# Experts of up to 128 slots: the whole first weight tile of the second product stays float32, not its first half alone

## The chip, the cores and the metric

The kernel runs on one core of a Trainium2 chip. The metric is device time in microseconds (us): the time of one execution, as a median over runs. The profile is one further execution, recorded by the hardware profiler; its times count from its first instruction. PE is the matrix engine (PEld its weight loads), ACT the activation engine, DVE the vector engine, POOL the engine that issues indirect DMAs, SP the one that issues the weight loads.

## What is computed

One layer of a trunk of 1024 tokens of width 1024: a mixer (a recurrence and an attention side by side) and then a mixture of 32 experts, of which each token takes four. The change lies in the experts alone. Their part of the reference, cut to the core:

```python
def expert_block(args):                       # one expert e, a block of its tokens
    tok, gate, e = args
    xb = xt[tok]
    hid = xb @ w1[e] + b1[e]                  # first product, 1024 -> 2 x 1024
    glu = jnp.minimum(hid[:, :1024], 7.0)
    lin = jnp.clip(hid[:, 1024:], -7.0, 7.0)
    act = glu * jax.nn.sigmoid(1.702 * glu) * (lin + 1.0)
    return (act @ w2[e] + b2[e]) * gate[:, None]   # second product, 1024 -> 1024
```

All of it is float32.

## The kernel before

**Tiles and units.** The 32 experts are taken in an order that alternates between well filled and thinly filled ones, so position j (0 to 31) has room for c slots: the even positions 168 down to 136, the odd positions 1 to 25 exactly 128 (thirteen of them), 27 to 31 136. An expert's weights are six tiles of 2 MB: four of w1 (w=1, q=0..3) and two of w2 (w=2, q=0 and 1). The tiles of two experts are interleaved: (j+1,1,0), (j,2,0), (j+1,1,1), (j,2,1), (j+1,1,2), (j+1,1,3), in the notation (position, w, q). They are loaded into four buffers `wraw0` to `wraw3` in turn, by SP, in that order (`w_load`, L1369; line L1380 for w1, L1386 for w2); a load waits until the last reader of the tile four places earlier is done. Each tile is worked off in two halves, h=0 and h=1; a half is a unit.

**Split and native units.** A float32 half tile is split for PE: ACT rounds it to `whi` (L1409, `w_hi`), DVE takes the rest, `wlo = wraw - whi` in bf16 (L1427, `w_lo`). `next_hi` runs three units ahead of PE, `next_lo` two. A unit of the first product (`first`, L1429) is 16 matmuls with `whi` (L1437) and 16 with `wlo` (L1441) into a PSUM tile `hid`, of which there are two; ACT and DVE empty it into `ht` (L1447, L1448). A split unit of the second product (`second`, L1498) is 12 matmuls of 512 columns: `whi` with the two parts `ah` and `al` of the activation, `wlo` with `ab`. `gated` makes `act` and these parts. A native unit (`native`) skips all of that: four matmuls in float32 straight from `wraw` and `act`, which PE runs as eight instructions. Before, the first half of the first w2 tile, (j,2,0) h=0, is native for every expert.

**The gather.** While PE works on an expert, the rows of the next one are found and fetched: one-hot rows times `aux` on PE (L1308), some small DVE steps on `sa` that end in the integer row numbers `si` (L1318), an indirect DMA on POOL into `xg` (L1327), and transposes `xt` on PE (L1344), which stand in PE's order behind unit (j+1,1,1) h=1 for position j+2.

**Order.** The program is recorded unit by unit (`experts`, L1555); a scheduler of the framework then sets the order on each engine, and each engine runs its list in that order. So an instruction that waits holds back all that stands behind it on its engine.

Of the kernel before, what the change touches and what calls it, by code (L numbers as in the profile page):

```python
# [67 lines left out]
def run(*gens):  # L68
    for g in gens:
        for _ in g:  # L70
            pass


class Box:
# [40 lines left out]
class Trunk:  # L115
# [798 lines left out]
    def mix(self, rp, zps, rps, sps, make_pool):  # L914
# [152 lines left out]
        self.ep0 = make_pool[1]()  # L1067
        bank = iter(("sbt", "sbo") * 4)
        run(self.x_transpose(self.xs[0], self.ep0, lambda: sps.tile([128, 512], FT, name="fxt", tag=next(bank), bufs=1)))
        self.next_lo(1)  # L1070
        self.next_hi(2)
# [322 lines left out]
    @staticmethod  # L1394
    def native(u):

        return u.t.w == 2 and u.t.q == u.h == 0

    def w_hi(self, u, pool):
        nc = self.nc  # L1400
# [49 lines left out]
    def gated(self, u, pool):  # L1450

        nc, x = self.nc, u.t.x
        c, part = x.c, 2 * (u.t.q // 2) + u.h
        n1 = self.rest(c)
        glu, lin = (t[:, 2 * u.h:2 * u.h + 2] for t in x.t)
        sg = pool.tile([128, 2, c], FT, name="hs", bufs=1, tag="hs")
        nc.scalar.activation(sg, glu, AF.Sigmoid, scale=ALPHA)
        nc.vector.tensor_scalar(lin, lin, LIMIT + 1.0, 1.0 - LIMIT, op0=OP.min, op1=OP.max)
        yield
        act = pool.tile([128, 2, 128 + n1], FT, name="act", bufs=5, tag="act")  # L1460
        if c < 128 + n1:
            nc.gpsimd.memset(act[:, :, c:], 0.0)
        nc.vector.scalar_tensor_tensor(lin, sg, SIG_MAX, lin, op0=OP.min, op1=OP.mult)
        nc.vector.scalar_tensor_tensor(act[:, :, :c], glu, LIMIT, lin, op0=OP.min, op1=OP.mult)
        x.act.append(act)
        if part == 0:
            x.parts.append(None)
            return
        ah = pool.tile([128, 2, 128], FR, name="ah", bufs=ABUF, tag="ah")
        ab = pool.tile([128, 2, 128], BF, name="ab", bufs=ABUF, tag="ab")  # L1470
        nc.scalar.activation(ah, act[:, :, :128], AF.Copy)
        nc.scalar.activation(ab, act[:, :, :128], AF.Copy)
        yield
        al = pool.tile([128, 2, 128], FR, name="al", bufs=ABUF, tag="al")
        nc.vector.tensor_tensor(al, act[:, :, :128], ah.bitcast(FT), op=OP.subtract)
        x.parts.append((ah, al, ab))

    def second(self, u, pool, psum):


        nc, x, t = self.nc, u.t.x, u.t
        first, last = t.q == u.h == 0, t.q == u.h == 1
        n1 = self.rest(x.c)
        nj = 128 // n1 if n1 else 0
        wd = D // nj if n1 else 0
        if first:
            x.ps = [psum.tile([128, 512], FT, name="ey", bufs=2) for _ in range(2)]
            if n1:
                x.pr = psum.tile([128, 512], FT, name="er", bufs=1)
        i = 2 * t.q + u.h  # L1490
        if self.native(u):
            products = [(x.act[i], t.raw, j) for j in range(2)]
        else:
            ah, al, ab = x.parts[i]
            products = [(a, u.hi, j) for j in range(2) for a in (ah, al)] + [(ab, u.lo, j) for j in range(2)]
        for m, (a, w, j) in enumerate(products):
            for n in range(2):
                nc.tensor.matmul(x.ps[n], a[:, j, :128], w[:, j, n * 512:(n + 1) * 512],  # L1498
                                 start=first and m == 0, stop=last and m == len(products) - 1)
        if n1 and u.h == 1:  # L1500
            for k in range(4):
                a = x.act[2 * t.q + k // 2]
                for g in range(nj):
                    nc.tensor.matmul(x.pr[g * n1:(g + 1) * n1, :wd], a[:, k % 2, 128:], t.raw[:, k, g * wd:(g + 1) * wd],  # L1504
                                     start=t.q == k == 0, stop=t.q == 1 and k == 3)
        if not last:
            return
        y = pool.tile([128, D], FT, name="ey", bufs=1)
        for n in range(2):
            ns = slice(n * 512, (n + 1) * 512)  # L1510
            nc.vector.scalar_tensor_tensor(y[:, ns], x.ps[n], x.gate[:, 0:1], self.g2b[:, ns], op0=OP.mult, op1=OP.mult)  # L1511
        rows = self.out.rearrange("b s d -> (b s) d")
        nc.gpsimd.indirect_dma_start(out=rows, out_offset=bass.IndirectOffsetOnAxis(ap=x.idx[:, 0:1], axis=0),  # L1513
                                     in_=y, in_offset=None, compute_op=OP.add)
        if n1:
            yr = pool.tile([128, wd], FT, name="yr", bufs=1, tag="yr")
            nc.vector.scalar_tensor_tensor(yr, x.pr[:, :wd], x.gate[:, 1:2], self.g2r[n1], op0=OP.mult, op1=OP.mult)
            rests = self.out.rearrange("b s (j d) -> (b s j) d", j=nj)
            nc.gpsimd.indirect_dma_start(out=rests, out_offset=bass.IndirectOffsetOnAxis(ap=x.idx[:, 2:3], axis=0),
                                         in_=yr, in_offset=None, compute_op=OP.add)  # L1520

    def load(self):

        pools = (self.wp, self.wp, self.ep1, self.ep2)
        while self.loaded < len(self.tiles) and (self.loaded < WRAW or self.loaded - WRAW in self.free):
            pool = pools[self.loaded % WRAW]
            if pool is None:
                return
            run(self.w_load(self.tiles[self.loaded], pool))
            self.loaded += 1  # L1530
# [193 lines left out]
def tile_trunk(ctx, tc, ins, out, dbg=None):  # L1724
# [11 lines left out]
    with ExitStack() as pre:  # L1736
# [21 lines left out]
                for tag in ("rwum", "rwT", "rwv", "rwk")]  # L1758
        ada = T.ada(0, sp, sps, iter(big).__next__, "sbt")
        run(take(ada, 8))  # L1760
        xt = next(norms[0])
        w = [T.z_weights(128 * m, zp) for m in (12,)]
# [87 lines left out]
```

## Time and profile before

| | |
|---|---|
| time before, median of 3 runs | 2486.65 us (2483.01 to 2488.38) |
| the profiled execution | 2474.98 us, span 2473.2 us |
| PE busy over the span | 2331.7 us (94%) |
| DVE, ACT busy | 1969.1 us (80%), 1576.0 us (64%) |
| granted PE clock, mean | 0.973 |
| time of one weight load, issue to landing, median | 14.5 us |

The experts fill the span from about 1085 us to the end. There PE is busy nearly all the time, and the loads keep the DMA engines busy too. A busy share is an average; which of the two ends last at a place is read from the waits and the chain.

### The profile page before, as it was taken

What the parts mean: (1) busy time and instruction counts of PE and PEld (TensorE: products, weight loads), DVE (VectorE), ACT (ScalarE), POOL (GpSimd) and SP (SyncE); (2) the same over time, 40 slices, a digit from 0 to 9 for tenths busy, and PEclk for the clock granted to TensorE, in tenths of its full rate; (3) what the DMA queues carried; (4) which work ended last, traced back from release to release, by engine and by line L of the source; (5) the groups of instructions that cost most, each with busy time, mean ns of one, the idle gap of its engine ahead of it and who ended that gap; (6) DMA issues with size and microseconds to landing.
All of it is one profiled execution on the core that took longest, in us unless ns stands there. A gap on an engine that the chain in (4) does not pass through costs nothing.

```text
span 2473.2 us, 49792 instructions
## 1 busy us (share of the span) xinstructions
PE 2331.7 (94%) x19973; PEld 1765.6 (71%) x19973; DVE 1969.1 (80%) x3639; ACT 1576.0 (64%) x2467; POOL 219.5 (9%) x182
## 2 busy tenths in 40 slices
PE   6889999999999799979999999999999999999997
PEld 2456666667676665667887787888788877877875
DVE  5567568669687768678888888989888889899875
ACT  3635556557666646346676676677777777776764
POOL 0000000000000000001121111111111111121111
PEclk9989999999999799979999999999999999999999
DMA  8773343332232312567898898899899999998995
GB/s 300 268 242 114 104 118 105 112 102 83 79 106 77 107 47 93 185 213 273 302 342 279 300 362 312 313 328 363 317 314 334 343 322 323 333 365 300 320 318 158
DMA packets 321006, 579.57 MB, mean 234 GB/s; under 512 B 46526, under 2 KB 110020, under 8 KB 320740
## 3 DMA queue, kind: packets, MB, share of 16 engines
q1 hardware_dynamic: 304768, 532.21, 60.6%
q0 software_dynamic: 14304, 43.53, 7.1%
q8 instruction: 159, 2.61, 0.4%
q10 hardware_dynamic: 1700, 0.61, 0.1%
q14 instruction: 75, 0.61, 0.1%
HBM read 517.69 MB, written 58.61 MB: 233 GB/s over the span
## 4 chain that ended last, share of the span: by engine, by line
PE 70%; DMA 14%; DVE 8%; ACT 5%; issue 3%; SPq 0%; POOL 0%; POOLq 0%; ACTq 0%; DVEq 0%
PE hid L1437 14%; PE ey L1498 14%; DMA wraw<-in_exp_w_dram 8%; PE hid L1441 6%; PE rwps L660 6%; PE zps L336 4%; PE zps L338 3%; PE zps L337 3%; PE er L1504 3%; PE sbo L526 2%; DMA xg<-h2d,si 2%; ACT whi L1409 2%; PE mp L972 1%; PE sbt L523 1%; PE mp L973 1%
## 5 line engine op out<-in xcount | busy, mean ns | idle before, releaser
L1409 ACT ACTIVATE whi<-wraw 128x2048 fp32r<-128x2048 f32 (+1 forms) x361 | 675.2, 1874 | 364.3 <-PE hid L1437 167.3
L1427 DVE TENSOR_TENSOR wlo<-wraw,whi 128x2048 bf16<-128x2048 f32 (+1 forms) x361 | 804.3, 2233 | 118.2 <-PE hid L1441 73.2
L1437 PE MATMUL hid<-X,whi 128*128 128x256 f32 (+7 forms) x4096 | 622.9, 304 | 27.1 <-DVE ht L1448 25.2
L1437 PEld LDWEIGHTS hid<-X,whi 128*128 128x128 f32 x4096 | 560.6, 191 | 62.2 <-issue 44.9
L1441 PE MATMUL hid<-xb,wlo 128*128 128x128 bf16 (+7 forms) x4096 | 300.6, 227 | 0.0
L1441 PEld LDWEIGHTS <-wlo 128*128 128x128 bf16 x4096 | 253.4, 98 | 18.3 <-issue 0.3
L338 PE MATMUL zps<-hhi,zwlo 128*128 128x512 f32 x416 | 247.1, 594 | 0.0
L336 PE MATMUL zps<-hhi,zwhi 128*128 128x512 f32 x416 | 188.8, 454 | 22.1 <-DVE zlast L380 9.6
L337 PE MATMUL zps<-hlo,zwhb 128*128 128x512 bf16 x416 | 168.5, 405 | 1.4 <-DVE hlo L247 1.4
L1447 ACT ACTIVATE ht<-hid,b1r 128x128 f32<-128x128 f32 (+7 forms) x496 | 156.8, 371 | 6.1 <-PE hid L1441 5.9
L1498 PE MATMUL ey<-whi,ah 128*128 128x512 f32 x384 | 142.2, 451 | 0.0
L1448 DVE TENSOR_TENSOR ht<-ht,hid 128x256 f32<-128x256 f32 (+7 forms) x256 | 114.1, 446 | 25.6 <-ACT ht L1447 25.0
L1513 POOL DMA_INDIRECT out_dram<-ey,si x32 | 91.5, 2859 | 410.6 <-DVE ey L1511 409.4
L336 PEld LDWEIGHTS zps<-hhi,zwhi 128*128 128x128 f32 x416 | 82.7, 199 | 54.8 <-issue 22.1
L1498 PE MATMUL ey<-wraw,act 128*128 128x512 f32 x256 | 121.4, 607 | 0.0
L1498 PE MATMUL ey<-whi,al 128*128 128x512 f32 x384 | 120.6, 395 | 0.0
L1327 POOL DMA_INDIRECT xg<-h2d,si x49 | 78.8, 1609 | 406.4 <-PE ey L1498 210.2
L337 PEld LDWEIGHTS <-zwhb 128*128 128x128 bf16 x416 | 42.2, 102 | 93.5 <-issue 88.9
L1498 PE MATMUL ey<-wlo,ab 128*128 128x512 bf16 x384 | 99.6, 382 | 0.0
L514 DVE TENSOR_TENSOR_SCAN se<-se 128x128 f32<-128x128 f32 (+3 forms) x96 | 92.8, 970 | 0.7
L244 ACT ACTIVATE zwhi<-zwraw 128x1024 fp32r<-128x1024 f32 x50 | 52.8, 1055 | 60.3 <-PE zps L336 40.4
L1498 PEld LDWEIGHTS ey<-whi,ah 128*128 128x128 f32 x384 | 69.9, 189 | 28.6 <-issue 14.8
(475 smaller groups left out, 4095.3 us busy)
## 6 DMA issues: line engine op xcount, KB each, us to landing
wraw<-in_exp_w_dram SPq DMA_DIRECT2D x189, 2048.0 KB, 14.5
zwraw<-in_w_in_dram SPq DMA_DIRECT2D x50, 512.0 KB, 4.1
aw<-in_ada_w_dram SPq DMA_DIRECT2D x32, 512.0 KB, 5.7
zr<-zo SPq DMA_DIRECT2D x28, 256.0 KB, 2.3
zs<-zo SPq DMA_DIRECT2D x24, 256.0 KB, 2.1
nx<-in_x_dram SPq DMA_DIRECT2D x8, 512.0 KB, 7.1
awh<-in_ada_w_dram SPq DMA_DIRECT2D x8, 512.0 KB, 4.6
mx<-in_x_dram SPq DMA_DIRECT2D x16, 256.0 KB, 3.2
```

Source lines behind the costliest of these rows:

```text
L336: nc.tensor.matmul(ps, hi[:, k], self.hhi[:, k, s], start=k == 0, stop=False)
L337: nc.tensor.matmul(ps, hb[:, k], self.hlo[:, k, s], start=False, stop=False)
L338: nc.tensor.matmul(ps, lo[:, k], self.hhi[:, k, s], start=False, stop=k == ND - 1)
L514: nc.vector.tensor_tensor_scan(er, er, er, initial=carry, op0=OP.add, op1=OP.bypass)
L660: self.nc.tensor.matmul(out[hs], lhsT[hs], rhs[hs], start=start, stop=stop)
L1409: nc.scalar.activation(dst[:, k], src[:, k], AF.Copy)
L1427: nc.vector.tensor_tensor(dst[:, k], src[:, k], hi[:, k], op=OP.subtract)
L1437: nc.tensor.matmul(ps[:, b, :2 * c], u.hi[:, k, b * 128:(b + 1) * 128], x.X2[:, k].rearrange("p a c -> p (a c)"), start=k == 0, stop=False)
L1441: nc.tensor.matmul(ps[:, b, :c], u.lo[:, k, b * 128:(b + 1) * 128], x.xb[:, k, :], start=False, stop=k == ND - 1)
L1447: nc.scalar.activation(dst[:, b], ps[:, b, c:2 * c], AF.Identity, bias=x.bias[:, f + b:f + b + 1])
L1448: nc.vector.tensor_tensor(dst, dst, ps[:, :, :c], op=OP.add)
L1498: nc.tensor.matmul(x.ps[n], a[:, j, :128], w[:, j, n * 512:(n + 1) * 512], start=first and m == 0, stop=last and m == len(products) - 1)
```

## The change

A new function `nat(c)` says how many halves of w2 stay native: two for an expert with up to 128 slots, one otherwise. For the thirteen odd positions 1 to 25, unit (j,2,0) h=1 becomes native: its `whi` on ACT, its `wlo` on DVE, the `ah`, `ab` (ACT) and `al` (DVE) of that quarter of the activation are not made, and its 12 matmuls become four float32 ones, eight instructions. The slice of `t.raw` picks the half of the tile.

```diff
+def nat(c):
+
+    return 2 if c <= 128 else 1
...
     def native(u):
 
-        return u.t.w == 2 and u.t.q == u.h == 0
+        return u.t.w == 2 and 2 * u.t.q + u.h < nat(u.t.x.c)
...
         x.act.append(act)
-        if part == 0:
+        if part < nat(c):
             x.parts.append(None)
             return
...
         if self.native(u):
-            products = [(x.act[i], t.raw, j) for j in range(2)]
+            products = [(x.act[i], t.raw[:, 2 * u.h:2 * u.h + 2], j) for j in range(2)]
```

Two places of the order, both around the second products of position 9 (128 slots) while position 10 (160 slots) has its first. ACT before; `wraw_16257` is tile (9,2,0), `wraw_16259` tile (10,1,1), the four `ht` of 128 columns empty the two units of (9,1,3):

```order
L1457 ACTIVATE hs<-ht 128x256
L1409 ACTIVATE whi<-wraw_16257 128x2048
L1447 ACTIVATE ht<-hid,b1r 128x128 x4
L1409 ACTIVATE whi<-wraw_16259 128x2048
L1471 ACTIVATE ah<-act 128x256
L1472 ACTIVATE ab<-act 128x256
L1457 ACTIVATE hs<-ht 128x256
L1447 ACTIVATE ht<-hid,b1r 128x160 x2
L1409 ACTIVATE whi<-wraw_16259 128x2048
```

ACT at the same place after the change, where tile (10,1,1) is `wraw_16181`:

```order
L1462 ACTIVATE hs<-ht 128x256
L1452 ACTIVATE ht<-hid,b1r 128x128 x4
L1462 ACTIVATE hs<-ht 128x256
L1476 ACTIVATE ah<-act 128x256
L1477 ACTIVATE ab<-act 128x256
L1414 ACTIVATE whi<-wraw_16181 128x2048
L1476 ACTIVATE ah<-act 128x256
L1477 ACTIVATE ab<-act 128x256
L1452 ACTIVATE ht<-hid,b1r 128x160 x2
L1414 ACTIVATE whi<-wraw_16181 128x2048
```

No `whi` stands ahead of the four `ht` any more; an `hs` and an `ah` and `ab` have moved ahead of the first `whi` of tile (10,1,1). DVE before, a little later, from the first `wlo` of tile (10,1,1) to the row numbers of the gather for position 11:

```order
L1427 TENSOR_TENSOR wlo<-wraw_16259,whi 128x2048
L1475 TENSOR_TENSOR al<-act,ah 128x256
L1463 SCALAR_TENSOR_TENSOR ht<-hs,ht 128x256
L1448 TENSOR_TENSOR ht<-ht,hid 128x320
L1464 SCALAR_TENSOR_TENSOR act<-ht 128x256
L1311 COPY sa<-xt 128x5
L1427 TENSOR_TENSOR wlo<-wraw_16259,whi 128x2048
L1475 TENSOR_TENSOR al<-act,ah 128x256
L1448 TENSOR_TENSOR ht<-ht,hid 128x320
...
L1296 TENSOR_SCALAR oh<-slot,keyr 128x160
L1316 TENSOR_TENSOR sa<-sa 128x1
L1318 CAST si<-sa 128x1
```

DVE there after the change:

```order
L1432 TENSOR_TENSOR wlo<-wraw_16181,whi 128x2048
L1453 TENSOR_TENSOR ht<-ht,hid 128x320
L1480 TENSOR_TENSOR al<-act,ah 128x256
L1432 TENSOR_TENSOR wlo<-wraw_16181,whi 128x2048
L1453 TENSOR_TENSOR ht<-ht,hid 128x320
L1316 COPY sa<-xt 128x5
L1301 TENSOR_SCALAR oh<-slot,keyr 128x160
L1319 SCALAR_TENSOR_TENSOR sa<-sa 128x1
L1320 TENSOR_TENSOR sa<-sa 128x1
L1301 TENSOR_SCALAR oh<-slot,keyr 128x160
L1321 TENSOR_TENSOR sa<-sa 128x1
L1323 CAST si<-sa 128x1
```

An `al` and the gating steps have moved ahead of this stretch; the copy of `sa` has moved behind both `wlo`, and one more `oh` stands ahead of `si`. On PE and SP the order is as before but for the replaced matmuls.

## Rows read from the trace of the kernel before

**Rows 1.** Busy time by window: busy us (count) of each engine, PE clock, DMA share, GB/s

```profile
1500.00:1600.00 100.00, 97.97 (x865) 81.44 (x864) 91.92 (x130) 73.24 (x102) 12.95 (x7) 1.00 0.93 326
```

**Rows 2.** Waits of PE, 1157 to 2202 us: total us, times, longest

```profile
PE hid L1437 <- DVE ht L1448: 22.6, 19, 2.7
PE xt L1344 <- DMA xg<-h2d,si: 3.2, 5, 1.1
```

**Rows 3.** Chain that ended last, in order of time: start, us, what

```profile
1506.21 11.15 DMA wraw<-in_exp_w_dram
1517.45 1.91 ACT whi L1409
1520.47 2.58 PE hid L1437 x16
...
1617.77 7.39 DMA xg<-h2d,si
```

**Rows 4.** Timeline of ACT: start, us, line, form, idle before and its releaser

```profile
1517.45 1.91 ACT L1409 ACTIVATE whi<-wraw 128x2048 fp32r<-128x2048 f32 x1 [2.53 <-DMA wraw<-in_exp_w_dram]
1519.27 1.12 ACT L1447 ACTIVATE ht<-hid,b1r 128x128 f32<-128x128 f32 x4
1522.77 1.92 ACT L1409 ACTIVATE whi<-wraw 128x2048 fp32r<-128x2048 f32 x1 [2.38 <-DMA wraw<-in_exp_w_dram]
...
1526.06 1.92 ACT L1409 ACTIVATE whi<-wraw 128x2048 fp32r<-128x2048 f32 x1
```

**Rows 5.** Timeline of DVE at the same place

```profile
1516.10 2.29 DVE L1427 TENSOR_TENSOR wlo<-wraw,whi 128x2048 bf16<-128x2048 f32 x1
1519.90 0.42 DVE L1448 TENSOR_TENSOR ht<-ht,hid 128x256 f32<-128x256 f32 x1 [1.51 <-ACT ht L1447]
...
1528.41 2.28 DVE L1427 TENSOR_TENSOR wlo<-wraw,whi 128x2048 bf16<-128x2048 f32 x1
1530.61 0.42 DVE L1475 TENSOR_TENSOR al<-act,ah 128x256 fp32r<-128x256 f32 x1
...
1531.72 0.15 DVE L1318 CAST si<-sa 128x1 int32<-128x1 f32 x1
```

**Rows 6.** Timeline of PE, positions 9 and 10

```profile
1520.47 2.58 PE L1437 MATMUL hid<-X,whi 128*128 128x320 f32 x16 [1.49 <-DVE ht L1448]
...
1527.73 3.68 PE L1498 MATMUL ey<-wraw,act 128*128 128x512 f32 x8
...
1533.81 2.70 PE L1437 MATMUL hid<-X,whi 128*128 128x320 f32 x16
...
1540.98 0.60 PE L1344 MATMUL xt<-ident,xg 128*128 128x128 f32 x4
1541.33 0.72 PE L1498 MATMUL ey<-whi,ah 128*128 128x512 f32 x2
...
1543.99 0.82 PE L1498 MATMUL ey<-whi,ah 128*128 128x512 f32 x2
```

**Rows 7.** The same PE rows in other pairs: first and last with a wait

```profile
1165.30 0.92 PE L1437 MATMUL hid<-X,whi 128*128 128x368 f32 x4 [1.75 <-DVE ht L1448]
...
2187.66 0.37 PE L1437 MATMUL hid<-X,whi 128*128 128x288 f32 x1 [1.12 <-DVE ht L1448]
...
1457.18 0.33 PE L1344 MATMUL xt<-ident,xg 128*128 128x128 f32 x1 [0.49 <-DMA xg<-h2d,si]
...
2209.01 0.44 PE L1344 MATMUL xt<-ident,xg 128*128 128x128 f32 x2 [1.64 <-DMA xg<-h2d,si]
```

**Rows 8.** Gather of 1532.66 us (for position 11), issue to landing

```profile
L1327 POOL DMA_INDIRECT xg<-h2d,si x1: 1004/1004/1004, 1532.7 to 1532.7; - x1
DMA to landing us min/median/max: 7.8/7.8/7.8
```

**Rows 9.** Gather of 1490.1 us (for position 10), and the DMA share around it

```profile
DMA to landing us min/median/max: 4.4/4.4/4.4
1487.00:1493.50 6.50, 6.50 (x55) 3.89 (x55) 5.92 (x14) 1.91 (x1) 3.14 (x2) 1.00 0.25 70
```

**Rows 10.** Issue of the load of tile (10,1,3) into the buffer of tile (9,2,0)

```profile
L1380 SPq DMA_DIRECT2D wraw<-in_exp_w_dram x1: 372/372/372, 1531.5 to 1531.5; - x1
```

## The prediction

> **What bounds the kernel now.** I read busy time by window first, then PE's waits, the chain that ended last, and the timeline of one pair of positions, 9 and 10. In the experts PE is busy 98 us of 100 while DMA stands at a share of 0.93 [rows 1], so both are near their limit and the waits must tell which one ends last. From 1157 to 2202 us, the stretch of the thirteen changed positions, PE waits 22.6 us for DVE's `ht` and 3.2 us for gathered rows [rows 2]; all the rest of PE's time is its own work. The reader should therefore count two things: PE work added or removed, which shows in full, and those few waits. Work taken off ACT or DVE is worth only what it takes out of a wait.
>
> The chain says where the waits come from [rows 3]: a weight load of 11.15 us, then ACT's `whi`, then PE, and in another pair a gather of 7.39 us. In the pair shown, ACT stands idle 2.53 us for tile (9,2,0), converts its second half at 1517.45, and only then, at 1519.27, gets to the four `ht` that stand behind it [rows 4]. DVE's `ht` comes at 1519.90 after 1.51 us of idling for ACT [rows 5], and PE, which needs that PSUM tile empty, starts unit (10,1,0) h=0 at 1520.47 after a wait of 1.49 us [rows 6]. The conversion that holds up the queue is the one that the change removes.
>
> The same row stands at the first unit of position j+1 in eleven of the thirteen pairs; the first has 1.75 and the last 1.12 us [rows 7], the sum is 17.92 of the 22.6 us. The other eight waits of that line (4.7 us) lie elsewhere, and the change doesn't touch them.
>
> **The change, part by part.**
>
> *PE.* From the native unit at 1527.73 to the next first product at 1533.81 there are 6.08 us for one native and one split unit; a split unit between two others takes 1541.33 to 1543.99, 2.66 us [rows 6]. A native unit is therefore 3.42 us, two are 6.84, and the change adds 0.76 us a pair, 13 x 0.76 = 9.9 us of PE work. Nothing hides it, as PE is the engine that all wait for, except where PE would wait anyway. The Trainium skill (FP8 and Floating Point Precision, TensorE Precision Notes) counts four passes for a true float32 product. By that the native unit is 16 passes of 512 columns against 12, a third more; 3.42 / 2.66 = 1.29 agrees, and a third of 2.66 over 13 units would make the term 11.5 us.
>
> *ACT and DVE.* They lose 13 x 1.91 us of `whi` [rows 4] and 13 x 2.29 us of `wlo` [rows 5], and three small steps each time. By itself this gives nothing. But the four `ht` no longer stand behind a `whi` that waits for tile (9,2,0). The next `whi` that waits for a load, 1522.77 [rows 4], stands behind the `ht` in the new order. What is late next for PE's first unit is DVE: the `wlo` from 1516.10 ends at 1518.39 [rows 5] and the `ht` of 0.42 follows, 1518.8, while PE would arrive at 1520.47 - 1.49 = 1518.98. So the wait goes entirely.
>
> *The tile itself.* PE now reads the second half of (9,2,0) directly, some 12 us after ACT had it; no wait there.
>
> *The gather.* PE's next stop is `xt` at 1540.98, and here the gain can be lost. The gather issued at 1532.66 lands 7.8 us later [rows 8], 1540.46: only 0.52 us before PE needs it. In the thirteen pairs six show a wait there, first 0.49, last 1.64 [rows 7], in all 4.85 us, and seven a slack of 0.04 to 1.20 us. The gather does not hang on PE but on the load: `whi` of tile (10,1,1) at 1522.77 when it lands, the two `wlo`, then `si` at 1531.72. A PE that comes earlier waits for it. So a pair's change is the PE term 0.76 - w - g (w the wait removed, g the wait at `xt` now), but never a gain of more than s + e, with s the slack and e how much earlier the gather lands.
>
> *How much earlier, e.* Two parts. Order: the second `wlo` starts at 1528.41 although its `whi` is ready at 1526.06 + 1.92 = 1527.98; the `al` and the gating ahead of it are gone or moved, so 0.43 earlier. Behind it the `al` of 1530.61 goes (about 0.3), while the copy and one `oh` come; I take 0.45 in all. Queue: the buffer of tile (9,2,0) is now read until the end of the second native unit. The load into it was issued at 1531.5 [rows 10], as the first native unit ended (1527.73 + 3.68). Now that end is 1527.73 - 1.49 + 6.84 + 0.25 = 1533.3, so the load comes 1.9 us later, and for that time the gather has less company. A gather at a DMA share of 0.25 takes 4.4 us [rows 9], against 7.8. Were 1.9 us of it run at the quiet rate, it would save 1.9 x (1 - 4.4/7.8) = 0.83; I take 0.35, as the load before it is still arriving. The sum is e = 0.8; the bounds are 0 (nothing of it comes through) and 1.6. The Trainium skill (DMA: Bandwidth & Descriptors, Queues, rings and completion order) has each DMA engine alternate between the queues with work, packet by packet. The two gathers agree.
>
> That later load is the part that could cost. The tiles behind it land up to 1.9 us later, too. But the loads of a pair already pause once: at 1487 to 1493.5 the DMA share is 0.25 [rows 9], as they wait there for a tile's last reader. What lands late before that can be made up. I put the cost at nothing; without the pause it would be up to 1.9 us in each of thirteen pairs.
>
> *The sum* (w, g or s read at the two PE rows of each pair as in rows 6 and 7; all us):
>
> | position | w | g | s | 0.76-w-g | change at e=0.8 |
> |---|---|---|---|---|---|
> | 1 | 1.75 | 0 | 0.37 | -0.99 | -0.99 |
> | 3 | 1.02 | 0 | 0.28 | -0.26 | -0.26 |
> | 5 | 2.67 | 0 | 1.20 | -1.91 | -1.91 |
> | 7 | 1.16 | 0.49 | 0 | -0.89 | -0.80 |
> | 9 | 1.49 | 0 | 0.52 | -0.73 | -0.73 |
> | 11 | 1.68 | 0.53 | 0 | -1.45 | -0.80 |
> | 13 | 0.96 | 0 | 0.24 | -0.20 | -0.20 |
> | 15 | 0 | 1.09 | 0 | -0.33 | -0.33 |
> | 17 | 1.95 | 0.22 | 0 | -1.41 | -0.80 |
> | 19 | 2.38 | 0 | 0.04 | -1.62 | -0.84 |
> | 21 | 1.74 | 0.88 | 0 | -1.86 | -0.80 |
> | 23 | 0 | 0 | 0.04 | +0.76 | +0.76 |
> | 25 | 1.12 | 1.64 | 0 | -2.00 | -0.80 |
>
> Together -8.5 us. With e = 0 it is -1.9, with e = 1.6 it is -12.2. Against the profiled execution of 2474.98 us (a span of 2473.2 and 1.8 around it) that is 2466.5; the median of the runs shown lies 11.7 us above that execution, so I forecast 2486.65 - 8.5 = 2478.1 us.
>
> **The rivals.**
>
> *The gather holds.* The waits go, and PE stands as long at `xt` instead. For it: thirteen of thirteen pairs have a slack of 1.2 us or less. Against it: the order shortens the path to `si`. It gives e = 0, -1.9 us, 2484.8.
>
> *The gather is no limit.* With the later load out of its way it lands early enough for nearly all, e = 1.6: 2474.4.
>
> *Slower: the wait moves to the next load.* The `whi` of tile (10,1,1) waits 2.38 us for its load already [rows 4], and with the `whi` before it gone, that is the first thing on ACT that waits. If it holds up an `ht` that PE needs, w stays as it is and 13 x 0.76 us shows in full: 2496.5. Against it: behind it stand the `ht` of (10,1,0), and PE needs that PSUM tile again only at 1533.81 [rows 6], while the `ht` would be done by about 1526. It decides when that load comes some 7 us later than now. The rule of four passes cited above would lead here by itself, if nothing came back.
>
> **How the numbers follow.** Chances: the forecast 0.52, the gather holds 0.28, no limit 0.10, slower 0.10. A measurement of this kernel can tell about 0.2%, 5 us, from no change. The forecast (-8.5) and no limit (-12.2) are faster by more than that, 0.62; the gather that holds lies within, 0.28; slower 0.10. The range goes from 2472 (no limit, less half the spread of the runs, 2483.01 to 2488.38) to 2487.5 (the gather holds, plus the same) and leaves out the slower case and the tails. The forecast's own range, e from 0.4 to 1.2, is 2476 to 2481 (-10.6 to -5.6).
>
> **What would show it.** After the change PE's wait for `ht` should fall from 22.6 to about 5 us, and its wait for gathered rows, 4.85 us in the thirteen pairs, stay near it: where a pair's PE column goes below its change, the difference is the new wait, 4.4 us in all. The two native units should take 6.8 us from their start to the next first product. ACT's `whi` of tile (j+1,1,1) should still start with the landing of its load, and `si` stand about 0.45 us nearer behind it than the 8.95 us between 1522.77 and 1531.72. The gather should take about 7.4 us where it took 7.8. Wrong would be: waits of `hid` for `ht` that stay; a gather that lands no earlier; new waits for loads in the second half of a pair, from the load that now starts 1.9 us later.

## The result and the profile after the change

The changed kernel takes 2499.66 us (2496.77 to 2503.67), the kernel before 2486.65 us beside it: a ratio of 1.006, 95% interval 1.004 to 1.008, slower by 13 us. The forecast was 2478.1 us with a range up to 2487.5. The profiled execution took 2503.03 us, its span is 2501.3 us.

I compare the two traces over one stretch, from PE's first unit of position 2 to its first unit of position 27, which holds the thirteen pairs: 1165.30 to 2229.10 before, 1170.59 to 2252.66 after, so 1063.8 and 1082.1 us, 18.3 us more. (The two measures of the loss, 18 and 13 us, need not agree better: the profiled execution of before was 11.7 us under its median, and over the fourteen profiles of this document the stretch begins between 1165.2 and 1175.6 us, though all edits lie in the experts.) Waits of PE in that stretch, after: total us, times, longest; those of before are [rows 2].

```profile
PE xt L1349 <- DMA xg<-h2d,si: 15.6, 7, 3.6
PE xt L1349 <- DVE wlo L1432: 5.7, 2, 3.1
PE hid L1442 <- DVE ht L1453: 4.2, 6, 2.5
PE xt L1349 <- DVE ht L1453: 3.4, 1, 3.4
PE xt L1349 <- DVE act L1469: 0.8, 1, 0.8
```

The wait for `ht` is down from 22.6 to 4.2 us, as forecast; in none of the thirteen pairs does the first unit of position j+1 wait any more (a pair is a position j of the thirteen and j+1; eleven had such a wait). But PE stands 25.5 us at `xt` (15.6 + 5.7 + 3.4 + 0.8), 4.8 us before. The releaser that such a row names is the one that came last by the record; `wlo`, `ht` and `act` have nothing to do with `xt`, and in each of these cases it was the gather. In pair 9 the timeline of PE now reads (start, us, idle before and its releaser; compare [rows 6]):

```profile
1528.99 2.59 PE L1442 MATMUL hid<-X,whi 128*128 128x320 f32 x16
...
1536.25 7.11 PE L1503 MATMUL ey<-wraw,act 128*128 128x512 f32 x16
1542.80 2.91 PE L1442 MATMUL hid<-X,whi 128*128 128x320 f32 x16
...
1550.96 0.63 PE L1349 MATMUL xt<-ident,xg 128*128 128x128 f32 x4 [0.61 <-DMA xg<-h2d,si]
```

From the first native unit to `xt` it was 13.25 us (1527.73 to 1540.98) and is 14.10 us without the wait (1550.96 - 1536.25 - 0.61): PE's added work is 0.85 us here, where the prediction had 0.76; read in the same way, it is 0.57 to 0.86 us over the thirteen pairs, 0.72 on average, 9.4 us together.

The gather is where the forecast went wrong. The landing of tile (j+1,1,1) shows in ACT's `whi`, from which `si` and the gather follow; first ACT, then DVE, then POOL of the same pair, to be held against [rows 4, 5, 8]:

```profile
1532.57 1.92 ACT L1414 ACTIVATE whi<-wraw 128x2048 fp32r<-128x2048 f32 x1 [1.73 <-DMA wraw<-in_exp_w_dram]
```

```profile
1540.74 0.15 DVE L1323 CAST si<-sa 128x1 int32<-128x1 f32 x1
1541.00 2.29 DVE L1432 TENSOR_TENSOR wlo<-wraw,whi 128x2048 bf16<-128x2048 f32 x1
1543.21 1.11 DVE L1301 TENSOR_SCALAR oh<-slot,keyr 128x160 bf16<-128x160 bf16 x6
```

```profile
1541.67 2.50 POOL L1332 DMA_INDIRECT xg<-h2d,si  x1 [11.72 <-issue]
```

And the landing of this gather:

```profile
DMA to landing us min/median/max: 9.2/9.2/9.2
```

`si` stands 8.17 us behind the `whi` (1540.74 - 1532.57), 8.95 before, so 0.78 us earlier. But POOL, which took 1.00 us for the gather, now takes 2.50 us, and the rows land 9.2 us behind its start where it was 7.8. From the `whi` to the landing it is 18.3 us (1541.67 + 9.2 - 1532.57), 17.7 before (1540.46 - 1522.77): the gather is 0.6 us late instead of 0.8 early. Twelve of the thirteen gathers take POOL 2.29 to 2.83 us, all thirteen 1.0 to 1.1 before; the thirteenth, for position 27 (136 slots), stays at 1.02. What is new beside POOL is on DVE: a `wlo` that starts 0.67 us ahead of POOL, where one-hot rows stood [rows 5]. It ends at 1543.29, and POOL ends 0.88 us later. The same holds in all twelve, within 0.85 to 0.9 us.

A second loss is in no step of the prediction. PE's clock by window: PE, PEld, DVE, ACT and POOL busy us (count), granted clock, DMA share, GB/s; first a wait at `xt` of pair 7, then what follows it:

```profile
1462.30:1465.50 3.20, 0.09 (x2) 0.03 (x1) 3.10 (x4) 1.83 (x4) 0.00 (x0) 1.00 1.04 396
1466.24:1469.65 3.41, 3.41 (x9) 2.14 (x9) 0.92 (x2) 1.22 (x3) 0.00 (x0) 0.50 1.06 392
1470.00:1476.00 6.00, 6.00 (x39) 4.89 (x38) 5.53 (x7) 4.34 (x5) 0.83 (x1) 1.00 1.01 380
```

And the timeline of PE there:

```profile
1465.50 0.63 PE L1349 MATMUL xt<-ident,xg 128*128 128x128 f32 x4 [3.12 <-DVE wlo L1432]
...
1467.45 1.05 PE L1503 MATMUL ey<-whi,ah 128*128 128x512 f32 x2
1468.30 1.05 PE L1503 MATMUL ey<-whi,al 128*128 128x512 f32 x2
...
1470.74 0.62 PE L1503 MATMUL ey<-whi,al 128*128 128x512 f32 x2
1471.21 0.62 PE L1503 MATMUL ey<-whi,ah 128*128 128x512 f32 x2
```

After 3.12 us without work PE ran 3.41 us at a granted clock of 0.50, the lower of its two levels: a pair of matmuls of 512 columns every 0.85 us instead of 0.47. In the stretch the records show 23.9 us at that level after the change and 13.7 before. If half of it is lost at half the rate, that is 5.1 us more, an estimate.

So the 18.3 us are: waits at `xt` +20.6, waits for `ht` -16.6 (of the 22.6 us before, 1.75 lie just ahead of the stretch, whose first unit ends that wait), low clock +5.1, and 9.2 that are left for PE's added work (0.71 us in each of thirteen pairs, beside the 0.72 read directly).

### The profile page after: what moved, and what is told of

Same layout as the page of the kernel before. It is cut to its first block, busy times and chain, and to the rows that moved or that the text cites. A ratio compares the mean times of both kernels' runs of the same rounds, so it can differ in the third digit from the quotient of the medians.

```text
span 2501.3 us, 49443 instructions
## 1 busy us (share of the span) xinstructions
PE 2352.9 (94%) x19766; PEld 1770.4 (71%) x19921; DVE 1941.4 (78%) x3613; ACT 1547.4 (62%) x2428; POOL 246.6 (10%) x182
## 4 chain that ended last, share of the span: by engine, by line
PE 68%; DMA 13%; DVE 10%; issue 4%; ACT 4%; SPq 0%; POOL 0%; POOLq 0%; ACTq 0%; DVEq 0%
PE hid L1442 14%; PE ey L1503 13%; DMA wraw<-in_exp_w_dram 7%; PE hid L1446 6%; PE rwps L665 6%; PE zps L341 4%; PE zps L343 4%; DMA xg<-h2d,si 3%; PE er L1509 3%; DVE wlo L1432 2%; PE zps L342 2%; PE sbo L531 2%; PE mp L977 1%; PE sbt L528 1%; ACT whi L1414 1%
## 5 line engine op out<-in xcount | busy, mean ns | idle before, releaser
L1432 DVE TENSOR_TENSOR wlo<-wraw,whi 128x2048 bf16<-128x2048 f32 (+1 forms) x348 | 775.4, 2232 | 165.7 <-PE hid L1446 88.4
L1414 ACT ACTIVATE whi<-wraw 128x2048 fp32r<-128x2048 f32 (+1 forms) x348 | 648.7, 1871 | 366.8 <-PE hid L1442 180.8
L1503 PE MATMUL ey<-wraw,act 128*128 128x512 f32 x360 | 165.8, 602 | 0.0
L342 PE MATMUL zps<-hlo,zwhb 128*128 128x512 bf16 x336 | 135.0, 402 | 1.4 <-DVE hlo L252 1.4
L1332 POOL DMA_INDIRECT xg<-h2d,si x49 | 93.8, 1914 | 426.2 <-PE ey L1503 200.5
L1453 DVE TENSOR_TENSOR ht<-ht,hid 128x256 f32<-128x256 f32 (+7 forms) x256 | 114.1, 446 | 13.8 <-ACT ht L1452 13.4
L1503 PE MATMUL ey<-whi,ah 128*128 128x512 f32 x332 | 124.4, 456 | 0.0
L1503 PEld LDWEIGHTS ey<-wraw,act 128*128 128x128 f32 x360 | 64.6, 190 | 64.0 <-issue 63.6
L1503 PE MATMUL ey<-whi,al 128*128 128x512 f32 x332 | 108.7, 409 | 0.0
L531 PEld LDWEIGHTS sbo<-sbv,sat 128*128 128x128 f32 x576 | 78.0, 198 | 19.3 <-ACT sat L529 9.5
L522 ACT ACTIVATE sc<-sc 128x128 f32<-128x128 f32 (+3 forms) x96 | 49.7, 521 | 65.2 <-DVE sc L521 64.5
```

What stands on the lines that cost most here:

```text
L342: nc.tensor.matmul(ps, hb[:, k], self.hlo[:, k, s], start=False, stop=False)
L531: nc.tensor.matmul(po[:, t % 4, h, :], at[:, b, :], v[:, c0 // 128 + b, hs], start=b == 0 and diag, stop=b == n - 1 and c0 == 0)
L1414: nc.scalar.activation(dst[:, k], src[:, k], AF.Copy)
L1432: nc.vector.tensor_tensor(dst[:, k], src[:, k], hi[:, k], op=OP.subtract)
L1453: nc.vector.tensor_tensor(dst, dst, ps[:, :, :c], op=OP.add)
```

## The experiments

Three theories for the loss at `xt`. A: the `wlo` that now stands behind `si` holds up POOL, as its end and POOL's go together. B: the gather is slowed by the weight load that starts later now. C: nothing of this matters, and the loss is PE's added work.

Each compares with runs of the kernel before on the same chip. "Stretch" is the one defined above, in the profiled execution; the two waits are PE's in it, and the last column is the time at a granted clock of 0.50 in it. "For `ht`" counts the wait that ends at the stretch's first unit, though the stretch begins behind it: 1.5 to 1.75 us in before, b_block, a_keep, b_two, b_one, b_early and b_front, nothing in the others.

| kernel | median us (before beside it) | ratio, 95% | stretch | for `ht` | at `xt` | low clock |
|---|---|---|---|---|---|---|
| before | 2486.65 | | 1063.8 | 22.6 | 4.8 | 13.7 |
| after | 2499.66 (2486.65) | 1.006, 1.004 to 1.008 | 1082.1 | 4.2 | 25.5 | 23.9 |
| a_clear | 2480.81 (2486.27) | 0.9971, 0.9951 to 0.9990 | 1058.0 | 4.4 | 12.0 | 3.4 |
| b_block | 2491.80 (2486.27) | 1.0026, 1.0008 to 1.0045 | 1069.7 | 28.8 | 4.8 | 13.7 |
| a_keep | 2518.57 (2486.27) | 1.0135, 1.0108 to 1.0161 | 1098.4 | 26.0 | 19.3 | 27.3 |
| a_early | 2472.91 (2486.27) | 0.9956, 0.9936 to 0.9977 | 1060.0 | 16.7 | 1.1 | 0 |
| b_two | 2509.43 (2486.68) | 1.0097, 1.0075 to 1.0119 | 1089.6 | 25.2 | 23.1 | 30.7 |
| b_one | 2481.01 (2486.68) | 0.9979, 0.9961 to 0.9998 | 1068.2 | 26.4 | 6.6 | 17.1 |
| b_early | 2468.88 (2486.68) | 0.9934, 0.9914 to 0.9954 | 1052.6 | 21.1 | 0 | 10.2 |
| b_order_early | 2485.46 (2486.68) | 0.9999, 0.9982 to 1.0015 | 1073.5 | 30.8 | 1.7 | 20.5 |
| a_front | 2469.74 (2483.54) | 0.9934, 0.9912 to 0.9956 | 1053.6 | 6.5 | 4.1 | 6.8 |
| b_front | 2479.56 (2483.54) | 0.9981, 0.9965 to 0.9996 | 1064.3 | 25.6 | 1.7 | 17.1 |
| a_front27 | 2469.08 (2481.49) | 0.9951, 0.9932 to 0.9971 | 1046.1 | 6.3 | 0.9 | 0 |
| a_front_all | 2466.23 (2481.49) | 0.9936, 0.9916 to 0.9957 | 1046.2 | 6.8 | 0.8 | 0 |

**a_clear: the `wlo` moved away from `si`.** The changed kernel; the next position's one-hot rows are recorded with the gather, and the `wlo` is tied behind them in DVE's order. It covers the twelve gathers for positions 3 to 25 and leaves out position 27's. In pairs 3 to 19 that `wlo` is the only thing that moves; in pair 1 an `ht` goes with it, in pairs 21 and 23 the second `wlo` of (j+1,1,1) too.

```diff
                 if t.q == 0 and 1 <= x.j < NE - 1:
-                    self.rows(xs[x.j + 1], pool, psum, u.h)
+                    y = xs[x.j + 1]
+                    if u.h or not hasattr(y, "oh"):
+                        self.rows(y, pool, psum, u.h)
+                    if u.h and y.c <= 128 and x.j + 2 < NE:
+                        self.hold = self.rows(xs[x.j + 2], pool, psum, 0)
...
+        late = self.hold if (u.t.w, u.t.q, u.h) == (2, 1, 0) else None
+        with self.tc.issue_after(late) if late else ExitStack():
```

> The changed kernel with one edit: in the thirteen pairs the wlo of unit (j,2,1) h=0, which stands right behind si on DVE, is put behind the next position's one-hot rows, where it stood before the change; all other rows on all engines keep their order. Theory A (that wlo reads two SBUF tiles and holds up POOL's gather, which ends 0.87 us behind the wlo's end): POOL's gather takes 1.0 us again where it took 2.3 to 2.8, lands 1.3 to 1.8 us earlier, and the waits of PE for gathered rows in the pairs, 25.4 us, fall by the smaller of wait and delay, 13.4 us together: about 2486 us, the time of the kernel before. Theory B (the gather is slowed by the weight load that now starts 1.9 us later): POOL may be quicker, the gather lands when that load does, and the time stays near 2500. Theory C (the loss is PE's added work of 13 x 0.76 us): no change, 2500.

DVE in pair 9, then POOL:

```profile
1539.12 0.14 DVE L1324 CAST si<-sa 128x1 int32<-128x1 f32 x1
1539.18 1.11 DVE L1301 TENSOR_SCALAR oh<-slot,keyr 128x160 bf16<-128x160 bf16 x6
1540.21 2.28 DVE L1435 TENSOR_TENSOR wlo<-wraw,whi 128x2048 bf16<-128x2048 f32 x1
```

```profile
1540.05 1.00 POOL L1333 DMA_INDIRECT xg<-h2d,si  x1 [11.90 <-PE ey L1508]
```

ACT's `whi` of tile (10,1,1) there, and the gather's landing:

```profile
1530.97 1.92 ACT L1415 ACTIVATE whi<-wraw 128x2048 fp32r<-128x2048 f32 x1 [3.55 <-DMA wraw<-in_exp_w_dram]
```

```profile
DMA to landing us min/median/max: 7.5/7.5/7.5
```

The `wlo` is as long and still runs beside POOL, but starts 0.16 us behind it, and POOL takes 1.00 us. The rows land 7.5 us behind POOL's start. PE's waits at `xt` fall from 25.5 to 12.0 us, by 13.4 as expected, and the low clock from 23.9 to 3.4 us, worth another 10.2. Of the 12.0 us, 3.95 are for position 27. The time is 18.9 us under that of the changed kernel and 5.5 us under that of before.

Not all of the 13.4 us need be the hold's. In pairs 7 to 19 the rows land 6.3 to 7.9 us behind POOL's end in a_clear and 6.0 to 7.9 in the changed kernel, and the waits there fall from 14.9 to 8.1 us; in the other five covered pairs they land sooner, too, 3.4 to 5.0 us behind POOL's end. Theory C is out as the main cause, since PE's added work is still there. So is theory B: from POOL's end to the landing it takes 6.7 us before and 6.6 after the change, as a mean of the twelve pairs. The rows take no more time on their way; they set out later.

**b_block: the same order made in the kernel before.** The one-hot rows tied behind that `wlo`.

```diff
+        if (u.t.w, u.t.q, u.h) == (2, 1, 0) and 1 <= u.t.x.j <= 25 and u.t.x.j % 2:
+            self.hold = last.ins
...
+        late, self.hold = getattr(self, "hold", None), None
+        with self.tc.issue_after(late) if late else ExitStack():
```

> The kernel before with one edit: in the thirteen pairs the next position's one-hot rows go behind the wlo of unit (j,2,1) h=0, so that this wlo stands right behind si on DVE, as in the changed kernel; nothing is native that was not. Theory A: POOL's gather goes from 1.0 to about 2.4 us and lands 1.4 us later; PE's waits for gathered rows grow by 1.4 less the slack of each pair, 13 x 1.4 - 2.7 = 15.5 us: about 2502. Theories B and C (nothing about POOL matters, since neither the load nor PE's work is changed): 2487, as before.

It did not make the case it was meant to make. Here ACT's `whi` comes later, and the `wlo` starts behind POOL where it still meets the gather, in pair 7 by 0.12 us (DVE, then POOL):

```profile
1459.92 0.15 DVE L1320 CAST si<-sa 128x1 int32<-128x1 f32 x1
...
1460.98 2.29 DVE L1429 TENSOR_TENSOR wlo<-wraw,whi 128x2048 bf16<-128x2048 f32 x1 [0.84 <-PE ey L1502]
```

```profile
1460.86 1.00 POOL L1329 DMA_INDIRECT xg<-h2d,si  x1 [13.88 <-PE ey L1502]
```

POOL keeps its 1.00 us, and the waits at `xt` their 4.8 us. So this says nothing against theory A; it shows that a `wlo` that starts 0.12 us behind POOL need not hold it up (in pair 25 one that starts 0.02 us behind did not either, 1.01 us). The 5.5 us that it lost are waits for `ht`, 28.8 instead of 22.6.

**b_two and b_one: the suspect by itself.** One DVE instruction added behind `si` in the kernel before, in the same place and of the same length; the order on every engine is the same in both. The diff is cut, and shows both added lines; each kernel has one of them.

```diff
+            g = self.g2b[:, None, :].to_broadcast([128, 2, D])
+            with self.tc.issue_after(si.ins):
+                nc.vector.tensor_tensor(self.spare, g, g, op=OP.mult)             # b_two
+                nc.vector.tensor_reduce(self.spare1, g, axis=AX.X, op=OP.add)     # b_one
```

> The kernel before with one added DVE instruction right behind si in the thirteen pairs, a TENSOR_TENSOR of 128x2048 that reads a constant tile in SBUF through both inputs and writes a tile that nobody reads. Theory A (a DVE instruction with two SBUF inputs that is under way when POOL begins the gather holds it up until 0.87 us behind its end): it starts about 0.85 us ahead of POOL and takes 2.3 us, so POOL's gather takes 2.3 us where it took 1.0, and lands 1.3 us later than in b_one. Over thirteen pairs, less the 2.7 us of slack, up to 14 us slower than b_one. Rival (it is DVE's time and not the port): POOL takes the same in both, and the two times agree.

> The kernel before with one added DVE instruction right behind si in the thirteen pairs, as in b_two and in the same order on all engines, but a TENSOR_REDUCE of 128x2048 that reads one SBUF tile. Theory A: POOL's gather keeps its 1.0 us. What this run is slower than before, 0 to some 8 us, is the price of 2.2 us of DVE in each pair. Rival: POOL's gather is as long as in b_two.

DVE and POOL in pair 9 of b_two:

```profile
1543.42 2.28 DVE L1322 TENSOR_TENSOR spare<-g2b 128x2048 bf16<-128x2048 f32 x1
...
1544.29 2.29 POOL L1331 DMA_INDIRECT xg<-h2d,si  x1 [11.70 <-issue]
```

And in b_one:

```profile
1532.83 2.27 DVE L1322 TENSOR_REDUCE spare<-g2b 128x2 f32<-128x2048 f32 x1
...
1533.70 1.00 POOL L1331 DMA_INDIRECT xg<-h2d,si  x1 [12.44 <-issue]
```

Both start 0.87 us ahead of POOL and last 2.3 us. With two inputs POOL ends at 1546.58, 0.88 us behind the instruction's end; with one it takes 1.00 us. This is theory A, with DVE's time held equal. The two instructions also differ in what they write, 2048 columns and 2. That this is not it, b_early shows (its edit is below; DVE, then POOL): an `ht` that reads one input from PSUM and writes 320 columns is under way when POOL begins, ends at 1452.59, and POOL does not wait for it.

```profile
1452.11 0.48 DVE L1448 TENSOR_TENSOR ht<-ht,hid 128x320 f32<-128x320 f32 x1
```

```profile
1452.32 1.00 POOL L1327 DMA_INDIRECT xg<-h2d,si  x1 [8.88 <-issue]
```

In a_early an `act` that reads both inputs from SBUF, and is no longer than that `ht`, does hold it; POOL ends 0.88 us behind it:

```profile
1526.23 0.42 DVE L1469 SCALAR_TENSOR_TENSOR act<-ht 128x256 f32<-128x256 f32 x1
```

```profile
1526.27 1.26 POOL L1332 DMA_INDIRECT xg<-h2d,si  x1 [7.78 <-issue]
```

The stretch is 21.4 us longer in b_two: 16.5 of waits at `xt` (14 expected), 6.8 of low clock, 1.2 less for `ht`. The medians differ by 28.4 us; of what exceeds 21.4 the traces show only that b_two's stretch began 6.9 us later, ahead of any edit.

**a_keep: PE's added work alone.** `next_hi`, `next_lo` and `gated` treat unit (j,2,0) h=1 as split again; `second` still takes it as native.

> The changed products alone: unit (j,2,0) h=1 is native, but its whi, wlo, ah, ab and al are still made, and nobody reads them. PE's added work shows without the rest. With the price of the prediction, 0.76 us a pair: ht waits stay at 22.6 us and the gather at 7.8 us, and the pairs that wait for the gather absorb part of it: between +6.4 us (the gather lands where it did) and +9.9 us (all shifts together), 2493 to 2497. If the loss of the change is all PE's work (theory C): 2500.

It is 32 us slower than before, far outside both expectations, and not for PE's work. With the unread `whi` and `wlo` in the program the scheduler made another order on DVE, in which `si` comes later: in pair 9 a third `wlo`, that of (9,2,1) h=0, stands between the small steps of the search and `si`.

```profile
1545.23 0.16 DVE L1320 TENSOR_TENSOR sa<-sa 128x1 f32<-128x1 f32 x1
1545.42 2.29 DVE L1437 TENSOR_TENSOR wlo<-wraw,whi 128x2048 bf16<-128x2048 f32 x1
...
1547.70 0.14 DVE L1323 CAST si<-sa 128x1 int32<-128x1 f32 x1
```

POOL takes 1.02 us, but starts later by that `wlo`, and PE waits 19.3 us at `xt` beside the 26.0 for `ht`. Against before the stretch is 34.6 us longer: 14.4 at `xt`, 3.6 for `ht` inside it, 6.8 of low clock, 9.8 left for PE's work, 0.75 us a pair. The total says nothing of that work, then; it shows once more what a late gather costs.

**a_early and b_early: the gather off the path.** Both kernels with the search and the gather recorded two units earlier.

```diff
-                if t.q == 0 and 1 <= x.j < NE - 1:
-                    self.rows(xs[x.j + 1], pool, psum, u.h)
+                if t.q == 0 and x.j == 1:
+                    self.rows(xs[2], pool, psum, u.h)
+                if t.q == 3 and 1 <= x.j < NE - 2:
+                    self.rows(xs[x.j + 2], pool, psum, u.h)
```

> The changed kernel with the gather taken off the path: the search for the rows of position j+2 and their gather are recorded at unit (j,1,3) instead of (j+1,1,0), two units earlier, from position 3 on. If the gather is where the change lost its gain (theories A and B): PE's waits at xt go in all pairs, and the sum of the prediction without that limit holds, 9.9 - 17.9 - 4.85 = -12.9 us against before: about 2474. Theory C: PE's added work is the loss and the gather is not, 2490 or more.

> The kernel before with the gather taken off the path as in a_early, nothing else. PE's waits for gathered rows (7.4 us in all, 4.85 in the thirteen pairs) go, its 22.6 us of waits for ht stay: 2479 to 2482. Rival: time won ahead of xt is lost again behind it, 2486.

The waits at `xt` go, but for 1.1 us in a_early. The change with an early gather, 2472.9 us, is 26.8 us under the change without; that far theory A or B is right, and C wrong. But the total came out as forecast by another road: the waits for `ht` are back at 16.7 us. DVE's longest wait in a_early's stretch tells what is new there (total us, times, longest):

```profile
DVE si L1323 <- DMA out_dram<-yr,si: 89.9, 12, 8.7
```

There are three buffers for the row numbers `si`, and in twelve pairs DVE stands 6.3 to 8.7 us at the early `si` until a scatter of an earlier position, which still reads the old ones, is done; all that stands behind it on DVE comes later, `ht` too. b_early has one such wait in its stretch, of 1.9 us. b_early came out 10 us better than expected; its stretch is 11.2 us shorter than that of before, of which waits (4.8 and 1.5) and low clock (1.7) explain 8. The rest stays open. The two times, 2472.9 with the change and 2468.9 without, don't show what the change is worth when the gather is early, since only one of the two kernels stands at `si`.

**b_order_early: the wait for `ht` removed without the float32 products.** b_early, with ACT's `whi` of (j,2,0) h=1 tied behind the last `ht` of (j,1,3) h=1.

```diff
+        late = u.t.x.ht if (u.t.w, u.t.q, u.h) == (2, 0, 1) else None
+        with self.tc.issue_after(late) if late else ExitStack():
```

> b_early, and ACT's whi of unit (j,2,0) h=1 put behind the last ht of unit (j,1,3) h=1, for every expert. It removes the 17.9 us of waits for ht that the change removed, without its float32 products. If the price of these products is the 0.76 us a pair of the prediction, this is a_early less 9.9 us, 2463; if a_early's products cost PE nothing that shows, it is 2473 like a_early. Rival: the later whi makes a later wlo, and PE waits there; 2475 or more.

The time is the rival's, 2485, but the wait is not: PE waits 0.9 us for `wlo` and 30.8 for `ht`, and the gain of b_early is gone. DVE stands at `si` here as in a_early, 76.7 us in twelve waits. In pair 9 (DVE, then PE):

```profile
1532.20 0.15 DVE L1318 CAST si<-sa 128x1 int32<-128x1 f32 x1 [6.80 <-DMA out_dram<-yr,si]
...
1538.60 0.88 DVE L1450 TENSOR_TENSOR ht<-ht,hid 128x320 f32<-128x320 f32 x2
```

```profile
1539.23 1.98 PE L1439 MATMUL hid<-X,whi 128*128 128x320 f32 x10 [2.08 <-DVE ht L1450]
```

So the run moved more than the wait that it was to remove, and what a later `whi` alone would cost stays open.

**a_front and b_front: `si` ahead of the second `wlo`.** The edit of a_clear, but the `wlo` that is tied behind the one-hot rows is that of (j+1,1,1) h=1; only DVE's order moves (and one row of ACT). It, too, leaves out position 27.

```diff
+        late = self.hold if (u.t.w, u.t.q, u.h) == (1, 1, 1) else None
```

> The changed kernel with one edit in DVE's order alone: in the thirteen pairs the second wlo of tile (j+1,1,1) goes behind the gather's small steps, si and the next one-hot rows. So nothing with two SBUF inputs of that length stands behind si, and si comes some 2.3 us earlier than in a_clear. If the gather is all that held the change back, the 12.1 us that PE still waits at xt in the thirteen pairs of a_clear go, and 1.7 us of low clock behind them: 2481 - 13.8 = 2467. Rival: the wlo that is now late stops PE at unit (j+1,1,1) h=1, and the time stays at 2481 or more.

> The kernel before with the same edit in DVE's order. Here only 4.9 us of waits at xt can go in the thirteen pairs, and the 23 us of waits for ht stay: 2480 to 2482. The difference between this run and a_front is then what the change is worth by itself where the gather is no limit: -18.3 us of waits for ht against +8 to +10.5 us of PE work, and the low clock behind the waits, -8 to -15 us. Rival (the change is worth nothing even then, since the waits for ht go elsewhere): the two agree within 4 us.

PE's waits in the stretch, a_front, then b_front:

```profile
PE hid L1447 <- DVE ht L1458: 6.5, 8, 1.8
PE xt L1350 <- DMA xg<-h2d,si: 4.1, 1, 4.1
```

```profile
PE hid L1442 <- DVE ht L1453: 25.6, 20, 3.2
PE xt L1345 <- DMA xg<-h2d,si: 1.7, 2, 1.5
```

Where the gather is early enough in both kernels, the change takes the time from 2479.56 to 2469.74 us, 9.8 us; the forecast for the change was 8.5. The stretch is 10.7 us shorter: 17.5 less for `ht` inside it, 2.4 more at `xt`, 5.1 less of low clock, 9.5 more for PE's work, 0.73 us a pair.

**a_front27 and a_front_all: the gathers left out.** The same edit for position 27 (136 slots) too, and for all positions. The last two lines are of one kernel each.

```diff
-                    if u.h and y.c <= 128 and x.j + 2 < NE:
+                    if u.h and (y.c <= 128 or y.j == 27) and x.j + 2 < NE:    # a_front27
+                    if u.h and x.j + 2 < NE:                                  # a_front_all
```

> a_front with its edit made for one gather more, that of position 27 (pair 25), which has 136 slots and was left out there. In a_front PE waits 4.08 us for it, the only wait for gathered rows that is left in the stretch, with 3.41 us of low clock behind it. Both theories of the gather: that wait goes, and the time falls by 4.1 and about 1.7 us, to 2464 to 2466. Rival: the four small copies and the two-part gather of that position keep si late, 2470.

> a_front with its edit made for all positions, the even ones of more than 128 slots too. In the pairs of even positions PE does not wait at xt, so that nothing is won there beyond a_front27: 2464 to 2466. If the wlo that goes back there holds up ht, PE's waits for ht grow and it is slower than a_front27.

The wait of 4.1 us and the low clock go, and the stretch of a_front27 is 7.5 us shorter than that of a_front (5.8 expected); the median shows only 0.7 us of it, and against the kernel before beside each, a_front27 is no better (12.4 us under it, a_front 13.8). a_front_all has the lowest time of all, 2466.23 us, 0.64% under the kernel before; a_front, a_front27 and b_early lie so close that their intervals don't part them. It is faster than the kernel before and than the changed one.

## Why the prediction was wrong

The step that failed is "How much earlier, e". It let the gather land 0.8 us earlier, with 0 as the lower bound. In pair 9 it lands 0.6 us later, and in a_clear, which differs by one place in DVE's list, it lands 1.1 us earlier (`whi` at 1530.97, landing at 1540.05 + 7.5, so 16.6 us against 17.7). In this pair both parts of e were about right in size: `si` came 0.78 us earlier (0.45 forecast), and without the hold the gather takes 7.5 us where it took 7.8 (0.35 forecast). In seven of the thirteen pairs e can't be read in this way, as the `whi` from which it counts started without a wait before the change. What the step left out is the price of what stands behind `si` on DVE. The new order has a `wlo` where the one-hot rows had been, one place behind the end of the list shown with the change, and I took POOL's 1.0 us [rows 8] over unchanged; the bound below was set at "nothing comes through" with no reason that excluded a loss.

*Why POOL waits.* Shown is this: a DVE instruction with two inputs in SBUF that is under way when POOL begins an indirect DMA delays POOL's end to 0.85 to 0.9 us behind its own, be it a `wlo` or the added TENSOR_TENSOR of 2.3 us, or an `act` of 0.4 us; a TENSOR_REDUCE of 2.3 us with one input does not, nor an `ht` with its second input in PSUM (b_early), nor one-hot rows (a_clear). A `wlo` that starts 0.12 us behind POOL does not hold it. Nearer to POOL's start the recorded times don't decide: an `act` 0.02 us ahead did not hold it in seven gathers of a_early, nor a `wlo` 0.02 us behind (b_block, pair 25), while in six gathers of b_order_early a `wlo` 0.05 us behind did, and the two-input instructions that followed without a gap did too; POOL took 6.41 to 6.42 us. Not shown is which part of the chip is shared. The Trainium skill (SBUF — State Buffer, Who interferes with whom, and Summary: rules for kernel authors) says that DVE reads its second SBUF input through an interface that it shares with GpSimd (POOL), and that whichever comes second waits for the whole instruction. By that rule the gather, which reads its row numbers, waits for the `wlo`; b_two, b_one and the 1.5 us of pair 9 agree, the six gathers of b_order_early do not by their start times. The first of these sections also tells of a `tensor_tensor` that was not seen to stall a DMA; the 2.29 to 2.83 us here say otherwise, and the measurement decides. The prediction did not hold that rule against the new order.

*PE's term.* 0.76 us a pair was about right: 0.72 from the first native unit to `xt`, as the mean of the thirteen pairs, and 0.71, 0.73 and 0.75 by the three sums over the stretch, 9 to 10 us where 9.9 were forecast. It does not all show where the prediction looked for it: from the first native unit to the next first product it is 6.55 us in pair 9 (1542.80 - 1536.25), where 6.84 were forecast and 6.08 were before.

*The wait for `ht`.* Right: gone in the eleven pairs that had it, 22.6 to 4.2 us over the stretch.

*The later load.* The issue of the load of tile (10,1,3) after the change (duration in ns, start in us):

```profile
L1385 SPq DMA_DIRECT2D wraw<-in_exp_w_dram x1: 372/372/372, 1543.4 to 1543.4; - x1
```

That is 1.7 us behind POOL's gather, where it was 1.2 us ahead of it [rows 8, 10]; I had counted 1.9 of these 2.9 us. It did no harm: PE's waits of the changed kernel and of a_clear name no load.

*The low clock.* Missing from the sum. With the change eleven waits for `ht` of 0.96 to 2.67 us went, and at `xt` eleven of 0.61 to 3.63 us stand where six stood. In the changed kernel eight waits of the stretch are over 2 us, and at the end of six of them (3.12, 2.04, 2.68, 3.05, 3.63 and 2.51 us) PE is at the lower level or soon falls to it. By the estimate above it made the loss 5 us larger and the repair 10 us better.

*The rivals.* "The gather holds" was nearest, and named the right place, but priced it as no gain where it is a loss. The rival on the other side, a `whi` that holds up an `ht`, did not happen.

*What was right, and what was luck.* Once nothing holds up POOL, the total: -8.5 us forecast, -5.5 measured in a_clear, and -9.8 between b_front and a_front. It is not right term by term. In a_clear PE waits 12.0 us at `xt`, in the sum 4.4, and the low clock, which the sum left out, gives back 5.1; between b_front and a_front it is 2.4 us more at `xt` against 5.1 of low clock. That the totals come near is in part luck. (At e = 0 the rows of the prediction's table add up to -1.83, not -1.9; nothing hangs on it.)

## What to carry to other kernels

When a change moves the order on DVE, look at what then runs at the moment when POOL begins each indirect DMA; a long instruction there with two inputs in SBUF costs its remaining time, and an instruction's duration in the old trace is a price only as long as its neighbours stay. A removed wait is worth what the next wait lets through, so find that one and move it first: here four edits of DVE's order, of a few rows each, decided between 13 us lost and 15 us won. Price a new wait with the clock that follows it.

## What the runs showed of the hardware that was not expected

- POOL's gather of 128 rows takes 1.00 us, and 2.29 to 2.83 us in the twelve pairs in which a `wlo` is under way at its start; beside two `wlo` in a row, back to back, one took 5.00 us, and ended 0.87 us behind the second (the second gather for position 27, before; DVE, then POOL). The two overlap by 0.07 us, and POOL was not let in between.

```profile
2202.79 4.47 DVE L1427 TENSOR_TENSOR wlo<-wraw,whi 128x2048 bf16<-128x2048 f32 x2
```

```profile
2203.13 5.00 POOL L1327 DMA_INDIRECT xg<-h2d,si  x1 [0.30 <-DVE oh L1296]
```

- A chain of two-input instructions holds it longer still: 6.42 us in b_order_early, pair 9, where POOL ended 0.88 us behind the fifth of them.
- 2.3 us of DVE work added in each of thirteen pairs (b_one) cost little: its stretch is 4.4 us longer than before and its median 5.7 us under the kernel before, though DVE is busy 80% of the span; the same time in another form (b_two) puts the median 23 us above.
- Behind some of its longer waits PE ran 3.41 us at the lower of its two clock levels, once 6.83 us. At half the rate 3.41 us cost up to 1.7 us beyond the wait itself, an estimate.
